# One token tile of four run ahead in plain float32 through the first half of a decoder block and gathered beside the rest; two tiles left dense

## The chip, the cores and the metric

One core of a Trainium2 chip. The time is the device time of one execution in microseconds. TensorE multiplies (a 128 x 128 array), VectorE and ScalarE work on 128-row tiles, GpSimd issues indirect DMAs (gathers of rows by an index), SyncE issues plain DMAs. Each engine runs its instructions in the order of the program and waits on semaphores for the others.

## The reference

512 tokens of width 1024 go through one block. The first half: adaLN modulation, an input projection to 7168 columns, four-head retention in chunks of 128 tokens, a spatial gating branch in chunks of 128, two output projections merged by gates, `w_out`, and the residual. The second half is PEER: each token picks 128 of 16384 experts (8 heads x 16) by two rounds of top-16, and sums single-neuron experts.

```python
q = (hb @ w_q).reshape(T, PEER_HEADS, 2, PEER_HALF)
s = jnp.einsum('thpc,hpnc->thpn', q, sub_keys)
sub_s, sub_i = lax.top_k(s, K)
cand = (sub_s[:, :, 0, :, None] + sub_s[:, :, 1, None, :]).reshape(T, PEER_HEADS, K * K)
top_s, top_i = lax.top_k(cand, K)
...
ue = expert_u[expert]
act = jax.nn.gelu(jnp.einsum('td,thkd->thk', hb, ue), approximate=False) * g
ve = expert_v[expert]
return jnp.einsum('thk,thkd->td', act, ve)
```

A token tile is 128 tokens. Retention and gating look back only, so the first tile needs no other tile.

## The kernel before

**First half.** All projections run over all four token tiles. A weight unit is 128 x 1024 float32 (512 KB). `Stream` loads units in order through SyncE into five `raw` buffers and splits each into a rounded part `wh` (ScalarE, L84) and a rest `wl` (VectorE, L87); `unit_mm` (L346) then makes three matmuls for each product (`wh`, `wl` and the activations' two parts), which come to nearly full float32. In the mode `tr` the 512 tokens are the columns, in the mode `nat` 512 weight columns are, once for each token tile.

**Second half.** Two methods share PEER's tokens. Dense: for a token, all 16384 expert scores are computed. `ahead` (L890) takes a 128-expert chunk of `uT` in plain float32 and spills the activations to memory (`sd`), `u_mm` does some chunks later in split form. The chosen experts' weights are spread by one-hot products (`onehots`, `wmm`) into a table `wd`, and in the last loop `a_make` multiplies activations and weights and `v_mm` (L1384) multiplies the result with the chunk's `v` rows. Gathered: for a token tile, `gather` (L1235) fetches, for each of the 128 choices, one `u` row and later one `v` row for all 128 tokens (512 KB each), and `consume` (L1251, L1256) does one VectorE pass over it, a dot product or an accumulation.

Before the change 320 tokens are dense (`TA`); the last tile (`accB`, 2 x 128 gathers) and 64 tokens of the first, folded into one 128-row set of 2 x 64 gathers (`accC`), are gathered: 384 in all, every one of them in the second half.

**What sets the order.** `plan()` writes the second half up to the last loop as a list of steps by estimated times of TensorE (`t["P"]`) and VectorE (`t["V"]`); `GPU` is the number of gathers credited for each ahead chunk. The last loop runs over 128 chunks in the list `items`; 88 have spilled scores, 40 are computed there. It spreads the gathers that are left (`left = NGT - ng[1]`) evenly over the iterations, with up to seven in flight, inside `a_make`, that is in VectorE's order ahead of the chunk's own work. The last four chunks are multiplied tile by tile, and each tile's norm and store follow.

Of the kernel before, what the change touches and what calls it, by code (L numbers as in the profile page):

```python
# [1 line left out]

# [21 lines left out]
H = 4  # L24
# [3 lines left out]
NA = 3  # L28
TP = 128 * NA
HC = 64  # L30
TA = TP - HC
# [6 lines left out]
GPU = 1.95  # L38
# [61 lines left out]
def plan():  # L100
# [4 lines left out]
    t = {"P": 0.0, "V": 0.0, "n": 0, "credit": 0.0, "go": False}  # L105

    def ahead():
        while pend and pend[0][0] <= t["P"]:
            _, st, c = pend.pop(0)
            steps.append(st)  # L110
            t["P"] += c
        steps.append(("U", t["n"]))
        t["n"] += 1
        t["P"] += 4.35
        if t["go"]:
            t["credit"] += GPU

    def pump():
        while (bq or dq) and t["V"] <= t["P"] + 6.0:
            if t["credit"] >= 1.0:  # L120
                t["credit"] -= 1.0
                steps.append(("gather",))
                t["V"] += 1.3
                continue
            st, c, after = (bq or dq).pop(0)
# [5 lines left out]
            if st[0] == "blist" and not t["go"]:  # L131
                t["go"], t["credit"] = True, -1.0
# [4 lines left out]
    def score(hp):  # L137
        steps.append(("score", hp))
        t["P"] += 0.9
        dq.append((("st1", hp), 3.2, None))  # L140
        if hp > 1 and hp % 2 == 0 or hp == 15:
            dq.append((("st2", (hp - 1) // 2), 2.7, None))
# [5 lines left out]
    ahead()  # L148
    ahead()
    steps.append(("chainB",))  # L150
    ahead()
    for g in range(4):
        for u in range(4):
# [3 lines left out]
            t["P"] += 5.2  # L157
# [8 lines left out]
    dq.append((("soft",), 4.0, None))  # L166
    for i in range(NA):
        dq.append((("list", i, 0), 3.4, None))
        dq.append((("list", i, 1), 4.2 if i else 4.8, (("listT", i), 0.8)))
# [15 lines left out]
def block_kernel(ctx: ExitStack, tc: tile.TileContext, a, out, dbg=None):  # L185
# [46 lines left out]

    big_p = ctx.enter_context(pool("big"))
    tmp2_cm = pool("tmp2"); tmp2 = tmp2_cm.__enter__()
    tmp_cm = pool("tmp"); tmp = tmp_cm.__enter__()

    def big(shape, dt, name):
        return big_p.tile(shape, dt, name=name, tag="big", bufs=6)
# [15 lines left out]
    def ada_dma(k, where=None, eng=None):  # L254

        ada_raw[k] = []
        for h in range(2):
            t = where[:, h] if where is not None else tmp.tile([128, 4, 256], F32, name="ada", tag="ada", bufs=4)
# [40 lines left out]
    def add_group(w, g):  # L299
        for u in range(4):  # L300
            ws.add(w[g, u])
# [16 lines left out]

# [20 lines left out]
    for i in range(PRE):  # L339
        ws.add(a["uT"][items[i][0]])  # L340
    for i in range(NCH):
        if PRE <= i + LA < NCH and items[i + LA][1]:
            ws.add(a["uT"][items[i + LA][0]])
        ws.add(a["v"][items[i][0] * 128:(items[i][0] + 1) * 128, :])

    def unit_mm(mode, u, wH, wL, sH, sL, targets, dds=(0, 1)):  # L346
# [5 lines left out]
        for ps, b in targets:  # L352
            ab = slice(b * 128, (b + 1) * 128)
            for dd in dds:
# [6 lines left out]
                else:  # L361
                    T.matmul(ps, wH[:, dd, ab], sH[:, d, :], start=st, stop=False)  # L362
                    T.matmul(ps, wH[:, dd, ab], sL[:, d, :], start=False, stop=False)  # L363
                    T.matmul(ps, wL[:, dd, ab], sH[:, d, :], start=False, stop=sp)  # L364

    def gemm(mode, sH, sL, evict, hooks=None, tiles=(0, 1, 2, 3)):
        banks = {}
        for u in range(4):
# [16 lines left out]
    ada_dma(1, stage[0][:, 1], nc.sync)
    ws.dma(2)
    for k in range(2, 6):
        ada_dma(k, stage[k // 2][:, k % 2], nc.sync)
        if k < 5:
            ws.dma(k + 1)  # L390
    dummy = cp.tile([128, 1], F32, name="dummy")
# [4 lines left out]
    for t in range(NT):  # L396
        scr = tmp2.tile([128, D], BF16, name="scr4", tag="t2", bufs=5)
        A.activation(scr, xn[:, t, :], AF.Square, accum_out=ss[:, t:t + 1])
    rsqrt(cp, rs, ss, NT, 1.0 / D, "rq")
    for t in range(NT):  # L400
        if t % 2:
            A.activation(xn[:, t, :], xn[:, t, :], AF.Copy, scale=rs[:, t:t + 1])
        else:
            V.tensor_scalar(xn[:, t, :], xn[:, t, :], rs[:, t:t + 1], None, op0=OP.mult)

    hH = big([128, ND, S], F32R, "hH")
    hL = big([128, ND, S], F32R, "hL")
    wsT = tmp.tile([128, 4, 128], F32, name="wsT")
    bsb = tmp.tile([128, 4, 128], F32, name="bsb")
    rope = tmp.tile([128, NT, 2, 64], F32, name="rope")  # L410

    def xT(d):
        ps = bank()
        for t in range(NT):
            T.transpose(ps[:, t * 128:(t + 1) * 128], xn[:, t, d * 128:(d + 1) * 128], ident)
        return ps

    def to_hT(d, ps):
        w = tmp2.tile([128, S], F32, name="ht", tag="t2", bufs=5)
        A.activation(w, ps, AF.Identity, bias=mod[:, 0, d:d + 1], scale=mod[:, 1, d:d + 1])  # L420
        A.copy(hH[:, d, :], w)
        V.tensor_tensor(hL[:, d, :], w, hH[:, d, :].bitcast(F32), op=OP.subtract)

# [6 lines left out]

    warm = bank()

    def warm_up(n):
        for _ in range(n):
            T.matmul(warm[:, 0:128], ones, ident, start=True, stop=True)
    warm_up(50)
# [23 lines left out]
    for d in range(ND):  # L460
        st_b(d + 1)
        st_a(d + 2)
        ws.split(d + 3)
        if d == 3:
            ws.dma(10)
        st_c(d + 1)
        if d == 0:
            banks0 = [(bank(), b) for b in range(4)]
            banks1 = [(bank(), b) for b in range(2)]
            ws.dma(6)  # L470
            for k in (6, 7):
                ada_dma(k, None, nc.sync)
                ws.dma(k + 1)
        if d % 2 == 0:
            wu = [ws.get(), ws.get()]
        for (wH, wL), bs in zip(wu, (banks0, banks1)):
            unit_mm("nat", d // 2, wH, wL, hH, hL, bs, dds=(d % 2,))
    lnr = big([128, 2, D], F32, "lnr")
    svg = big([128, NT, D], F32, "svg")
# [4 lines left out]
    nc.sync.dma_start(bsb, a["sgu_b"].to_broadcast([128, 512]).rearrange("p (g t) -> p g t", g=4))  # L484
    nc.sync.dma_start(gates[:, 0, :], a["b_ada"][2:3, :].to_broadcast([128, D]))
    nc.sync.dma_start(gates[:, 1, :], a["b_ada"][5:6, :].to_broadcast([128, D]))
    ws.dma(12)
# [6 lines left out]
    dump("hT", hH.bitcast(F32))  # L494
    dump("hTL", hL.bitcast(F32))
    for ps, b in banks0:
        ev_sv(0)(b, ps)
    for ps, b in banks1:
        ev_sv(1)(b, ps)
    gemm("nat", hH, hL, ev_sv(1), tiles=(2, 3))  # L500
# [22 lines left out]
    bgh = {u: [ada_bg] for u in range(4)}  # L523
# [3 lines left out]
    lrs = cp.tile([128, NT], F32, name="lrs")  # L527

    def ln_stats():
        for t in range(NT):  # L530
            st = tmp.tile([128, 2, 6], F32, name="st", tag="st", bufs=2)
            for i in range(2):
                V.bn_stats(st[:, i, :], svg[:, t, i * 512:(i + 1) * 512])
            V.bn_aggr(mv[:, t, :], st)
        rsqrt(cp, lrs, mv[:, :, 1], NT, 1.0, "rq")

    def ln_apply(t):
        v = svg[:, t, :]
# [4 lines left out]
    qk = big([128, 2, H, S], F32, "qk")  # L543

    def ev_rope(w):
        def f(b, ps):
            x = ps.rearrange("p (h d) -> p h d", h=H)
            x1, x2 = x[:, :, 0:64], x[:, :, 64:128]
            cb = rope[:, b, 0:1, :].to_broadcast([128, H, 64])
            sb = rope[:, b, 1:2, :].to_broadcast([128, H, 64])  # L550
# [9 lines left out]
            pend.append((w, b, r))  # L560
# [3 lines left out]
    def rope_tr():  # L564
        w, b, r = pend.pop(0)
# [3 lines left out]
        A.copy(qk[:, w, :, b * 128:(b + 1) * 128], ps.rearrange("p (h t) -> p h t", h=H))  # L569


# [3 lines left out]
    def mix(cc):  # L575
        g = cc // 2
        ps = bank()
        for t in range(NT):
            T.matmul(ps[:, t * 128:(t + 1) * 128], svg[:, t, cc * 128:(cc + 1) * 128], wsT[:, g, :],
                     start=True, stop=True)  # L580
        m = tmp2.tile([128, NT, 128], F32, name="mx", tag="t2", bufs=5)
        V.tensor_tensor(m, ps.rearrange("p (n t) -> p n t", n=NT), bsb[:, g:g + 1, :].to_broadcast([128, NT, 128]),
# [8 lines left out]
    def ev_u(g):  # L591
        def f(b, ps):
            cc = 4 * g + b
            u = tmp2.tile([128, S], F32, name="ug", tag="t2", bufs=5)
            A.activation(u, ps, AF.Gelu)
# [4 lines left out]
            if b == 3:  # L600
# [4 lines left out]
    gemm("nat", hH, hL, ev_rope(0), hooks={0: [ln_stats], 1: [lambda: ln_apply(0)], 2: [lambda: ln_apply(1)],  # L605
                                          3: [lambda: ln_apply(2)]})
# [1040 lines left out]
```

## Time and profile before

| | us |
|---|---|
| median of 3 runs | 1733.07 (1731.33 to 1735.44) |
| the profiled execution | 1731.39 |
| its span, first to last instruction | 1729.7 |
| TensorE busy | 1675.3 (97%) |
| VectorE busy | 1373.3 (79%) |
| ScalarE busy | 700.2 (40%) |
| GpSimd busy | 591.0 (34%) |

The stages by their first TensorE instruction: the dense first half to about 469 us, `w_out` and the second norm to 539, queries and ahead chunks to 880, one-hot products to 1068, then the last loop with its six prologue chunks, and from about 1686 us the last chunks and the final norm. The page's slices are of about 43 us each. DMA is the mean busy share of 16 DMA engines, beside it the bytes that they moved.

### The profile page before, as it was taken

The numbers are of one execution on the slowest core, as the hardware profiler recorded it, in microseconds if no ns is written. First come the engines' busy times: TensorE is split into PE (matmuls) and PEld (weight loads), VectorE is DVE, ScalarE is ACT, GpSimd is POOL, SyncE is SP. The second block draws the span as 40 slices with busy tenths as digits, with TensorE's granted clock in tenths as the row PEclk, the third lists the DMA queues.
The fourth block names the chain that finished last, engine by engine and source line by source line (L and its number), as shares of the span: only waits on it lengthen the run. The fifth ranks groups of instructions, "written<-read, shape, count | busy, mean of one in ns | idle before, by whom it ended". The sixth has DMA issues, their size and how long they took to land.

```text
span 1729.7 us, 23047 instructions
## 1 busy us (share of the span) xinstructions
PE 1675.3 (97%) x8029; PEld 1353.4 (78%) x8029; DVE 1373.3 (79%) x2712; ACT 700.2 (40%) x1140; POOL 591.0 (34%) x505
## 2 busy tenths in 40 slices
PE   9999999999999989999999988899999999999995
PEld 8888888888877877777777766788888888888873
DVE  7676763353553899999899977699999999899996
ACT  6532532234244343112357664334434444434334
POOL 0000110000000025666876554254444444454440
PEclk9999999999999999999999999999999999999997
DMA  9625662123334168999999999999999999999993
GB/s 376 239 98 171 228 222 74 61 85 103 120 125 154 60 214 327 410 396 409 350 357 381 400 392 389 363 368 393 381 398 379 407 391 381 405 382 396 372 354 116
DMA packets 138741, 502.83 MB, mean 291 GB/s; under 512 B 15648, under 2 KB 15680, under 8 KB 138496
## 3 DMA queue, kind: packets, MB, share of 16 engines
q0 software_dynamic: 70416, 259.85, 39.8%
q1 hardware_dynamic: 68208, 241.50, 36.9%
q8 instruction: 64, 1.05, 0.2%
q14 instruction: 53, 0.43, 0.1%
HBM read 460.89 MB, written 39.85 MB: 289 GB/s over the span
## 4 chain that ended last, share of the span: by engine, by line
PE 63%; DVE 24%; DMA 7%; issue 3%; ACT 2%; POOL 0%; SPq 0%; DVEq 0%; ACTq 0%; POOLq 0%
PE acc L1384 25%; PE mm L362 5%; PE mm L364 5%; PE mm L363 5%; PE mm L358 4%; PE mm L359 4%; PE mm L360 4%; DVE gw L1251 3%; PE mm L888 2%; PE mm L886 2%; PE mm L887 2%; DVE gwl L1251 2%; DVE gwh L1251 2%; DMA wd<-stg 2%; DMA gwl<-in_v_dram,eidx 2%
## 5 line engine op out<-in xcount | busy, mean ns | idle before, releaser
L87 DVE TENSOR_TENSOR wl<-raw,wh 128x1024 fp32r<-128x1024 f32 x268 | 326.0, 1221 | 143.1 <-ACT wh L84 140.0
L1384 PE MATMUL acc<-wh,ah 128*128 128x512 f32 x1280 | 375.8, 400 | 14.2 <-DVE ah L1365 14.2
L896 PE MATMUL mm<-h2F,raw 128*128 128x320 f32 (+2 forms) x1424 | 387.0, 432 | 0.0
L896 PEld LDWEIGHTS mm<-h2F,raw 128*128 128x128 f32 x1424 | 268.4, 191 | 107.3 <-issue 1.8
L84 ACT CAST wh<-raw 128x1024 fp32r<-128x1024 f32 x268 | 279.0, 1047 | 84.7 <-PE mm L360 39.4
L1384 PEld LDWEIGHTS acc<-wh,ah 128*128 128x128 f32 x1280 | 238.9, 189 | 78.3 <-issue 12.0
L1384 PE MATMUL acc<-wl,ah 128*128 128x512 f32 x768 | 244.7, 399 | 0.0
L1361 ACT CAST ah<-aw 128x320 fp32r<-128x320 f32 x128 | 59.0, 461 | 314.5 <-DVE aw L1359 310.7
L1384 PEld LDWEIGHTS acc<-wl,ah 128*128 128x128 f32 x768 | 145.9, 190 | 35.7
L1235 POOL DMA_INDIRECT gr<-in_v_dram,eidx x86 | 112.6, 1309 | 140.1 <-DVE accB L1256 122.1
L1235 POOL DMA_INDIRECT gr<-in_v_dram,ecidx x64 | 85.0, 1328 | 94.5 <-DVE wqb L1256 72.7
L1235 POOL DMA_INDIRECT gr<-in_u_dram,ecidx x64 | 83.6, 1306 | 88.4 <-DVE gr L1251 70.0
L1235 POOL DMA_INDIRECT gw<-in_u_dram,eidx x50 | 66.2, 1325 | 137.5 <-DVE eidx L1150 70.1
L1256 DVE SCALAR_TENSOR_TENSOR accB<-gr,dots,accB 128x1024 f32<-128x1024 f32 x86 | 110.2, 1281 | 1.3
L899 ACT ACTIVATE spl<-mm 128x320 f32<-128x320 f32 x88 | 38.0, 438 | 167.3 <-PE mm L896 105.2
L358 PE MATMUL mm<-wh,hH 128*128 128x512 f32 x256 | 102.3, 400 | 0.0
L888 PE MATMUL mm<-h2H,wl 128*128 128x320 f32 x320 | 98.9, 309 | 2.0 <-DVE wl L87 2.0
L886 PE MATMUL mm<-h2H,wh 128*128 128x320 f32 x320 | 98.9, 309 | 1.5 <-ACT wh L84 1.5
L360 PE MATMUL mm<-wh,hL 128*128 128x512 f32 x256 | 100.2, 391 | 0.0
L359 PE MATMUL mm<-wl,hH 128*128 128x512 f32 x256 | 100.2, 391 | 0.0
L887 PE MATMUL mm<-h2L,wh 128*128 128x320 f32 x320 | 98.9, 309 | 0.0
L1256 DVE SCALAR_TENSOR_TENSOR wqb<-gr,dotC,wqb 128x1024 f32<-128x1024 f32 x64 | 82.0, 1281 | 1.0
(343 smaller groups left out, 3148.6 us busy)
## 6 DMA issues: line engine op xcount, KB each, us to landing
raw<-in_uT_dram SPq DMA_DIRECT2D x128, 512.0 KB
raw<-in_v_dram SPq DMA_DIRECT2D x128, 512.0 KB
raw<-in_w_in_dram SPq DMA_DIRECT2D x60, 512.0 KB
wd<-stg POOLq DMA_DIRECT2D x10, 2048.0 KB
wqb<-wd SPq DMA_DIRECT2D x32, 640.0 KB
ada<-in_w_ada_dram POOLq DMA_DIRECT2D x28, 512.0 KB
sd<-spl POOLq DMA_DIRECT2D x44, 320.0 KB
sp<-sd SPq DMA_DIRECT2D x44, 320.0 KB
```

The source lines that it names most:

```text
L84: self.nc.scalar.copy(h, r)
L87: self.nc.vector.tensor_tensor(l, r, h.bitcast(F32), op=OP.subtract)
L358: T.matmul(ps, sH[:, d, ab], wH[:, dd, :], start=st, stop=False)
L359: T.matmul(ps, sH[:, d, ab], wL[:, dd, :], start=False, stop=False)
L360: T.matmul(ps, sL[:, d, ab], wH[:, dd, :], start=False, stop=sp)
L886: T.matmul(ps[:, p:q], h[:, d, :], h2H[:, d, cs], start=(d == 0), stop=False)
L887: T.matmul(ps[:, p:q], h[:, d, :], h2L[:, d, cs], start=False, stop=False)
L888: T.matmul(ps[:, p:q], l[:, d, :], h2H[:, d, cs], start=False, stop=(d == ND - 1))
L896: T.matmul(ps[:, p:q], r[:, d, :], h2F[:, d, HC + p:HC + q], start=(d == 0), stop=(d == ND - 1))
L1235: P.indirect_dma_start(out=r, out_offset=None, in_=a[tab], in_offset=bass.IndirectOffsetOnAxis(ap=ix[:, j:j + 1], axis=0))
L1256: V.scalar_tensor_tensor(acc, r, dt[:, j:j + 1], acc, op0=OP.mult, op1=OP.add)
L1384: T.matmul(accs[2 * t + e], x, y[:, e * 512:(e + 1) * 512], start=s0, stop=s1)
```

## The change

The first token tile goes alone through the first half before the other three. Its activations and the weights stay in plain float32: `gemm0` does one matmul for each product, with the tile's activations as stationary operand and 512 weight columns moving, on units that are not split. Its queries, scores and top-16 follow at once, and its gathers (2 x 128) are consumed by `bg_gather` after each weight unit of the other three tiles' first half (`GB1` = 1.4 each), and further on as before. The other tiles' first half has three tiles instead of four (`S3` = 384). In the second half two whole tiles are dense (`TA` = 256), the last tile is gathered as before, so there are 512 gathers. 80 chunks are spilled ahead and 48 computed in the last loop. Every second value chunk in the last loop stays unsplit (`vplain`) and is multiplied in plain float32. Weight units that the lone tile read are read again for the others.

```diff
-NA = 3
-TP = 128 * NA
-HC = 64
-TA = TP - HC
+N3 = NT - 1
+S3 = 128 * N3
+NA = 2
+TA = 128 * NA
...
-GPU = 1.95
+GPU = 1.4
+GB1 = 1.4
+VN = 2
...
-    t = {"P": 0.0, "V": 0.0, "n": 0, "credit": 0.0, "go": False}
+    t = {"P": 0.0, "V": 0.0, "n": 0, "credit": 0.0, "go": True}
...
+    add_two(a["w_in"][GSV:GSV + 2])
+    for g in (GSV, GSV + 1, GK, GQ, GV, GV + 1, GG, GG + 1, GU, GU + 1, GA, GA + 1):
+        add_group(a["w_in"], g, True)
...
+    vplain = [i % VN == 1 for i in range(NCH)]
...
+    def gemm0(s, evict, hooks=None, groups=2):
+
+        for g in range(groups):
+            ps = bank()
+            for u in range(4):
+                r = ws.get()
+                for dd in range(2):
+                    d = 2 * u + dd
+                    T.matmul(ps, s[:, d, :], r[:, dd * 512:(dd + 1) * 512], start=(d == 0), stop=(d == ND - 1))
+                for f in (hooks or {}).get((g, u), ()):
+                    f()
+            evict(g, ps)
...
+    gemm0(h0, ev_sv0, {(0, 1): [ada_bg], (0, 3): [ada_bg], (1, 1): [ada_bg]})
+    gemm0(h0, lambda g, ps: ev_rope(1, 0)(0, ps), {(0, 1): [ada_bg, lambda: ln_stats([0])], (0, 3): [lambda: ln_apply(0)]},
+          groups=1)
+    gemm0(h0, lambda g, ps: ev_rope(0, 0)(0, ps), {(0, 1): [ada_bg], (0, 2): [rope_tr]}, groups=1)
...
+    NGT = 4 * NJ
...
+        tab, j, G = ("u", "v")[i // NJ % 2], i % NJ, GT[i // (2 * NJ)]
...
+    def bg_gather():
+        if tq:
+            tq.pop(0)()
+        cr[0] = min(cr[0] + (0.6 if tq else GB1), 4.0)
+        gather_all()
+        while cr[0] >= 1.0 and ng[1] < ng[0]:
+            cr[0] -= 1.0
+            consume()
+            gather_all()
+    bg[0] = bg_gather
...
+    def v_mm(i, tiles, w, x, halves=(0, 1)):
         st, sp = (i == 0), (i == NCH - 1)
         for t in tiles:
-            if t == 0:
-                x = hl[:, TA:TA + 128]
-                runs = ((x, vh, st, False), (x, vl, False, sp))
+            o = slice(t * 128, (t + 1) * 128)
+            if vplain[i]:
+                runs = ((x[:, o], w, st, sp),)
             else:
...
-                runs = ((h, vh, st, False), (h, vl, False, False), (l, vh, False, sp))
+                h, l = x[:, 0, o], x[:, 1, o]
+                runs = ((h, w[0], st, False), (h, w[1], False, False), (l, w[0], False, sp))
```

On TensorE in the first half, at the value projection and the retention scores: before, all four tiles' split products (`hH`, `hL` are the two parts of the activations) go around the score products of all chunks.

```order
L358 MATMUL mm<-wh,hH 128x512
L359 MATMUL mm<-wl,hH 128x512
L360 MATMUL mm<-wh,hL 128x512
L651 MATMUL mm<-qk 128x512
L651 MATMUL mm<-qk 128x384
L651 MATMUL mm<-qk 128x256
L651 MATMUL mm<-qk 128x128
```

In the changed program the lone tile's piece of the same place stands some 800 instructions earlier, with unsplit units (`raw`) against the tile (`h`), its rotation (`rr`), scores (`qk`) and sums (`v`, `PT`) between them, and the sums of the modulation (`acc`).

```order
L416 MATMUL mm<-raw,h_104 128x512 x6
L632 MATMUL mm<-ident,rr 128x128 x4
L416 MATMUL mm<-raw,h_104 128x512 x4
L686 MATMUL mm<-qk_668 128x128 x4
L416 MATMUL mm<-raw,h_104 128x512 x6
L293 MATMUL mm<-ones,acc_905 128x1 x2
L416 MATMUL mm<-raw,h_104 128x512 x2
L698 MATMUL mm<-v_667,PT_953 128x256 x4
```

What moved: two matmuls stand for one weight unit where 24 stood, each unit is read a second time for the other three tiles, and each step of the tile follows the one before it closely.

On VectorE in the first half, at the gated output projection (`brb`) and the scores (`PT`): before, between the splits stand the modulation sums and the evictions.

```order
L273 TENSOR_TENSOR acc_2142<-acc_2142,acc_2143 128x256
L631 TENSOR_TENSOR brb<-mm,brb 128x512 x4
L87 TENSOR_TENSOR wl<-raw,wh 128x1024
L294 TENSOR_TENSOR gates<-mm,gates 128x256
L87 TENSOR_TENSOR wl<-raw,wh 128x1024 x3
L631 TENSOR_TENSOR brb<-mm,brb 128x512 x4
```

After, one or two gathered rows (`ga`, `gt`, `gwh`, `gwl` are the buffers; `h` the tile's activations) stand between one split and the next.

```order
L950 SCALAR_TENSOR_TENSOR gt,d_1824<-gt,h_1683 128x1024
L1078 TENSOR_TENSOR brb<-mm,brb 128x384 x4
L90 TENSOR_TENSOR wl<-raw,wh 128x1024
L950 SCALAR_TENSOR_TENSOR gwh,d_1824<-gwh,h_1683 128x1024
L90 TENSOR_TENSOR wl<-raw,wh 128x1024
L950 SCALAR_TENSOR_TENSOR gwl,d_1824<-gwl,h_1683 128x1024
```

What moved: gathers that the second half held stand here, 74 of them before the `w_out` projection of the three tiles.

On VectorE in the last loop: before, each chunk has one to three gathered rows among its own product (`aw`), rest (`ah`) and the splits of its weights.

```order
L1359 TENSOR_TENSOR aw<-sp_10854,wqb 128x320
L1251 SCALAR_TENSOR_TENSOR gr,dotC<-gr,h2C 128x1024
L1365 TENSOR_TENSOR ah<-aw,ah 128x320
L87 TENSOR_TENSOR wl<-raw,wh 128x1024 x2
L1359 TENSOR_TENSOR aw<-gs,wqb 128x320
L1251 SCALAR_TENSOR_TENSOR gr,dotC<-gr,h2C 128x1024 x3
L1365 TENSOR_TENSOR ah<-aw,ah 128x320
```

After:

```order
L1654 TENSOR_TENSOR aw<-sp_10577,wqb 128x256
L950 SCALAR_TENSOR_TENSOR gt,dB<-gt,h2B 128x1024 x2
L90 TENSOR_TENSOR wl<-raw,wh 128x1024
L1654 TENSOR_TENSOR aw<-gs,wqb 128x256
L950 SCALAR_TENSOR_TENSOR gt,dB<-gt,h2B 128x1024
L950 SCALAR_TENSOR_TENSOR gr,dB<-gr,h2B 128x1024 x3
L1665 TENSOR_TENSOR ah<-aw,ah 128x256
```

What moved: two to four rows stand in a chunk, every second chunk has no rest and no split of its value rows, and the loop begins with 202 of 512 gathers consumed, where it began with 170 of 384.

## Rows read from the trace of the kernel before

**Rows 1.** The page: span, busy us, DMA and bytes in 40 slices, packets.

```profile
span 1729.7 us, 23047 instructions
...
PE 1675.3 (97%) x8029; PEld 1353.4 (78%) x8029; DVE 1373.3 (79%) x2712; ACT 700.2 (40%) x1140; POOL 591.0 (34%) x505
...
DMA  9625662123334168999999999999999999999993
GB/s 376 239 98 171 228 222 74 61 85 103 120 125 154 60 214 327 410 396 409 350 357 381 400 392 389 363 368 393 381 398 379 407 391 381 405 382 396 372 354 116
DMA packets 138741, 502.83 MB, mean 291 GB/s; under 512 B 15648, under 2 KB 15680, under 8 KB 138496
```

**Rows 2.** Windows by stage: us, busy of each engine, clock, DMA share, GB/s.

```profile
60.00:469.00 409.00, 408.84 (x1879) 339.10 (x1878) 231.65 (x416) 137.04 (x191) 17.12 (x32) 1.00 0.37 127
539.00:880.00 341.00, 333.91 (x1372) 250.15 (x1371) 303.34 (x1215) 100.48 (x209) 167.61 (x145) 0.99 0.80 300
880.00:1068.00 188.00, 178.28 (x1154) 133.44 (x1152) 169.15 (x165) 120.24 (x134) 105.39 (x84) 0.99 1.01 384
700.00:820.00 120.00, 120.00 (x447) 84.72 (x446) 119.72 (x507) 21.94 (x63) 74.05 (x67) 1.00 1.02 404
1068.00:1686.00 618.00, 606.84 (x2923) 509.45 (x2924) 553.79 (x687) 248.49 (x454) 288.51 (x219) 1.00 0.99 384
1686.00:1730.00 44.00, 23.51 (x87) 17.40 (x85) 29.77 (x55) 19.50 (x35) 3.54 (x3) 0.78 0.33 115
```

**Rows 3.** Waits: engine, line, waited for, us, times, longest.

```profile
PE acc L1384 <- DVE ah L1365: 14.2, 9, 4.4
POOL gr L1235 <- DVE accB L1256: 131.9, 49, 16.4
```

**Rows 4.** TensorE: timeline (start, us), pieces of the chain, groups by form.

```profile
100.91 0.39 PE L364 MATMUL mm<-hH,wl 128*128 128x512 f32 x1
105.67 0.40 PE L364 MATMUL mm<-hH,wl 128*128 128x512 f32 x1
1200.27 0.31 PE L886 MATMUL mm<-h2H,wh 128*128 128x320 f32 x1
1202.33 0.31 PE L888 MATMUL mm<-h2H,wl 128*128 128x320 f32 x1
112.43 1.78 PE mm L579 x16
271.09 2.16 PE mm L651 x8
1150.29 15.18 PE acc L1384 x64
L1208 PE MATMUL mm<-ohA,ohB 128*128 128x128 f16 x320 | 39.2, 218 | 3.8 <-ACT stg L1210 1.6 <-ACT spl L899 1.5 <-DVE ohA L1193 0.7
```

**Rows 5.** DMA issues: count, KB each.

```profile
raw<-in_uT_dram SPq DMA_DIRECT2D x128, 512.0 KB
ada<-in_w_ada_dram POOLq DMA_DIRECT2D x28, 512.0 KB
wqb<-wd SPq DMA_DIRECT2D x32, 640.0 KB
sp<-sd SPq DMA_DIRECT2D x44, 320.0 KB
```

**Rows 6.** VectorE groups by form: busy us, mean ns, idle before.

```profile
L87 DVE TENSOR_TENSOR wl<-raw,wh 128x1024 fp32r<-128x1024 f32 x268 | 326.0, 1221 | 143.1 <-ACT wh L84 140.0
L1256 DVE SCALAR_TENSOR_TENSOR accB<-gr,dots,accB 128x1024 f32<-128x1024 f32 x86 | 110.2, 1281 | 1.3
L1256 DVE SCALAR_TENSOR_TENSOR wqb<-gr,dotC,wqb 128x1024 f32<-128x1024 f32 x64 | 82.0, 1281 | 1.0
L1251 DVE SCALAR_TENSOR_TENSOR gr<-gr,h2C 128x1024 f32<-128x1024 f32 x64 | 76.0, 1219 | 0.0
```

**Rows 7.** A window in which TensorE idles, columns as in rows 2.

```profile
640.00:680.00 40.00, 35.00 (x142) 26.14 (x141) 36.79 (x166) 13.98 (x32) 22.27 (x20) 0.91 0.80 278
```

More of the change, by code (lines that the diff above doesn't have):

```diff
@@ L1 @@
 from contextlib import ExitStack
+from types import SimpleNamespace
 import numpy as np
@@ L493, in block_kernel @@
     ws.ra, ws.sa = 5, 3
[L494 to L500, printed above, removed]
+    for g in range(2):
+        for ps, b in banks[g]:
+            ev_sv(g)(b, ps)
     ada_next = [8]
@@ new lines, in block_kernel, with ev_v0, scores0 @@
+    gemm0(h0, lambda g, ps: ev_rope(0, 0)(0, ps), {(0, 1): [ada_bg], (0, 2): [rope_tr]}, groups=1)
+    def ev_v0(g, ps):
+        A.copy(v0[:, half(g)], ps)
+    def scores0():
+        ps = bank()
+        for h in range(H):
+            T.matmul(ps[:, h * 128:(h + 1) * 128], qk0[:, 1, h, :], qk0[:, 0, h, :], start=True, stop=True)
+        PT0 = tmp2.tile([128, H, 128], F32, name="PT0", tag="t2", bufs=5)
+        V.tensor_tensor(PT0, ps.rearrange("p (h t) -> p h t", h=H), dec0, op=OP.mult)
+        PT["0"] = PT0
@@ new lines, in block_kernel, with pv0 @@
+    PT = {}
+    gemm0(h0, ev_v0, {(0, 0): [ada_bg], (0, 3): [rope_tr], (1, 1): [scores0]})
+    def pv0():
+        for hp in range(2):
+            ps = bank()
+            for hh in range(2):
+                h = 2 * hp + hh
+                T.matmul(ps[:, hh * 256:(hh + 1) * 256], PT["0"][:, h, :], v0[:, h * 256:(h + 1) * 256], start=True, stop=True)
+            A.copy(z0[:, half(hp)], ps)
+            for hh in range(2):
+                st = tmp.tile([128, 2, 6], F32, name="st", tag="st", bufs=2)
+                V.bn_stats(st[:, 0, :], ps[:, hh * 256:(hh + 1) * 256])
+                V.bn_aggr(hmv0[:, 2 * hp + hh, :], st[:, 0, :])
@@ new lines, in block_kernel, with score0 @@
+    l0 = lists_of(tk0, 1)
+    l0.e, l0.mx = (tk0.tile([128, 512], F32, name=n) for n in ("be", "bmx"))
+    s0 = {}
+    q0 = {}
+    def score0(g):
+        q = q0.pop(g)
+        ps = bank()
+        for i in range(4):
+            hp = 4 * g + i
+            kk_ = (keys0.a if hp < 8 else keys0.b)[:, hp % 8, :]
+            T.matmul(ps[:, i * 128:(i + 1) * 128], q[:, i * 128:(i + 1) * 128], kk_, start=True, stop=True)
+        s = (X[3], X[5])[g // 2][:, half(g % 2)]
+        A.copy(s, ps)
+        s0[g] = s
@@ L753, in ev_ret @@
         return f
+    gfree += [t0_tile("gt") for _ in range(2)]
     for g in range(2):
         gemm("tr", zH, zL, ev_ret(g))
+        if not g:
+            gdrop += ga + ["wh", "wl"]
+            gfree[:] = [b for b in gfree if not dropped(b)]
+    while any(dropped(b) for _, b in gt_t.values()):
+        consume()
+        gather_all()
+    bg[0] = lambda: None
     dump("mH", mH.bitcast(F32))
@@ L1323, in block_kernel @@
     dump("wd", wd)
-    while ng[1] < ng[0]:
+    gfree[:] = [x for x in gfree if not isinstance(x, str)]
+    gdrop += ["wh", "wl"]
+    while any(isinstance(b, str) for _, b in gt_t.values()):
         consume()
     ws.sa = 3
-    gfree, gdrop = [], []
     wx_cm.__exit__(None, None, None)
```

952 lines of the change are left out of this document (557 added, 395 removed).

## The prediction

> **What bounds the kernel now.** I read the page's busy shares and its forty slices first, then the windows of each stage, then the waits of the last stage, and only then single instructions. The page shows TensorE busy 97% of the span, with VectorE at 79%; the DMA line is what to look at: it is low from the second to the fourteenth slice and at nine tenths or more from the seventeenth to the last but one [rows 1]. The windows say the same by stage [rows 2]. In the dense first half (60 to 469 us) TensorE has no gap, VectorE works 232 of 409 us and the DMA engines run at a share of 0.37. From 700 to 820 us VectorE is busy 119.72 of 120 us and the DMA share is 1.02 at 404 GB/s. In the last loop (1068 to 1686 us) TensorE is busy 607 of 618 us, VectorE 554, and the DMA share is 0.99 at 384 GB/s. The waits there agree: TensorE lost 14.2 us to VectorE and nothing that is ascribed to a DMA, while GpSimd waited long for VectorE to free the buffer of the next gather [rows 3]. So TensorE sets the pace of the last loop, and the queues are full beside it without holding it up: two resources are at their end at once, a third close to it.
>
> **What TensorE saves and pays.** Prices first. A split matmul (three products of rounded operands) of 512 columns starts every 0.227 us (21 steps in 4.76 us), one of 320 columns every 0.147 us (14 steps in 2.06 us); a column is then worth (0.227 - 0.147) / 192 = 0.00042 us. Plain float32, which the trace records as two instructions for each matmul, costs about four times that a column: four score products of 1280 columns in all took 2.16 us, 0.00169 us a column; of 128 columns, eight took 1.78 us, 0.2225 us each. In the last loop a split product takes 15.18 / 64 = 0.237 us. A pair of one-hot products takes 39.2 / 320 = 0.12 us [rows 4].
>
> Up to the query projection (539 us before): in the split projections one token tile of four goes. 240 products of 512 columns disappear (54.4 us), 960 shrink from 512 to 384 columns (51.0 us). The lone tile adds 160 plain products of 512 columns (18 half-matrices of eight, and the two of the output projection): 160 x 512 x 0.00169 = 138.4 us, 128 plain query products of 128 columns, 28.5 us, and some 7 us of transposes and small products net. The two ahead chunks there shrink by 1.7 us. 539 - 105.4 + 138.4 + 28.5 + 7.0 - 1.7 = 606 us.
>
> What can be added to that: while the tile runs alone, it eats a weight unit of 512 KB every 1.73 us, 72 units, and 28 pieces of the modulation weights of the same size come through GpSimd's queue [rows 5]: 52.4 MB in about 139 us, 377 GB/s. The 404 GB/s of [rows 2] covers that, barely. Its steps also depend on each other: the key rotation waits on VectorE behind layer-norm work, and the routing of this tile lands on VectorE beside the first split gate group. Lower bound nothing; upper, weights at only the 300 GB/s of the query stage, 52.4 / 0.300 = 175, or 36 us, and some 10 more. I take 20 us: nearer the low end, since the rate needed is below what a row shows. So 626 us.
>
> The query and ahead stage with the one-hot stage (539 to 1068, 529 us): 86 ahead chunks of 2560 columns become 78 of 2048 (372 - 270 = 102 us saved), 384 projection products lose 128 columns (20.4 us), 16 score products (3.6 us) and 64 one-hot pairs (7.8 us) go: 134 us less, 395 us, with the waits of before kept. VectorE must follow: it worked 303 + 169 = 472 us there, of which 170 gathered rows at about 1.25 us [rows 6] were 212; 126 are left now (157 us), and of the other 260 I take a fifth off for the tile that left, 208: 365 us of 395. It fits. The DMA need (122 gathers, 94 units, the spilled activations and the expert weights) is 142 MB, 359 GB/s. It fits too. The last loop then begins at 626 + 395 = 1021 us.
>
> **The last loop.** TensorE's own part falls: 48 score chunks of 24 products at 256 columns (0.1205 us, 139 us), 64 split value chunks of 12 products (182 us), 64 plain ones of 4 (0.865 us each, 221 us): 542 us against the 607 of before. But the changed program, as built, has consumed only 74 gathers when the dense first half ends and 202 when the last loop begins; it leaves 310 of 512 to the last loop, where the kernel before left 214 (86, 64 and 64 in the groups of [rows 6]). The bytes: value rows 128 x 0.524 = 67.1 MB, score rows 48 x 0.524 = 25.2, expert weights 32 x 0.524 = 16.8, spilled activations 40 x 0.262 = 10.5, gathers 310 x 0.524 = 162.5, together 282 MB. The same count for the kernel before gives 67.1 + 21.0 + 21.0 + 14.4 + 112.2 = 236 MB, and 236 MB in 618 us is 381 GB/s, which the row confirms with 384. What rate will 282 MB get? Between the 384 of that loop and the 410 of the page's fullest slice: 734 to 688 us. I take 400, near the 404 of the window with a share of 1.02, since the loop of before also has stretches in which TensorE did not ask for more: 705 us. VectorE's part is 310 gathers at 1.27, 112 splits at 1.22 and some 77 us of small work, 608 us; so neither compute engine is the bound any more, the queues are. Gathers come late, VectorE stands behind them in order, the splits behind that stand, and TensorE waits. The TensorE time saved in this loop buys nothing.
>
> The Trainium skill (DMA: Bandwidth & Descriptors, Bandwidth) gives two ceilings, 435 GB/s for the ports and about 358 GB/s for memory to one core, and says that the second binds for loads. The 404 GB/s over 120 us speak against the second. By 358 the loop would take an estimated 788 us and the kernel end near 1856; by 435, 648 us and 1716.
>
> After the last gather the kernel before needed 44 us (1686 to 1730) for the last products, norm and store; the changed one has four chunks of two tiles there in place of three, and the same chain behind; I keep 44.
>
> **The sum.** 606 + 20 + 395 + 705 + 44 = 1770 us of span. The profiled execution took 1731.39 us for a span of 1729.7, and the median of the runs shown is 1733.07, so 3.4 us are added: **1773 us**, 2.3% slower. The gain of the design is real up to the last loop (47 us earlier); the loop then takes 87 us longer. A difference under 0.2% (3.5 us) could not be told from none.
>
> **Rivals.** *The queues are not the limit* (faster). Nothing before waits for a DMA in the loop, so 384 and 404 GB/s may be what was asked for and no ceiling, and the share near 1 only counts packets that wait for each other. Then VectorE paces the loop with 608 us: 606 + 20 + 395 + 608 + 44 = 1673, about 1676 us. It decides from 282 / (1730 - 1065) = 424 GB/s on; at that rate the kernel comes out even. For it: no DMA wait in [rows 3]. Against it: no slice of the page goes above 410, in stretches where different engines pace. The 435 of the Trainium skill would be this case.
>
> *The lone tile starves* (slower still). If units come at more than 1.73 us each, because five buffers and a second queue beside them do not give 377 GB/s, or the chain of one tile leaves TensorE waiting on VectorE at each step, the front pays 50 to 60 us where I put 20: 1803 to 1815 us. For it: plain chunks of 512 columns have no other tiles to hide a late eviction. Against: VectorE and ScalarE have half their time free there [rows 2].
>
> *TensorE's clock.* In the loop TensorE will idle about a quarter of the time. From 640 to 680 us it was busy 35 of 40 us and the granted clock was 0.91 of full speed [rows 7]; 542 us at 0.91 are 596, still under 705, so nothing changes. The Trainium skill (TensorE: Matmul & The Clock Gate, Part 1: The HAM clock gate) says that an idle array falls to 1.2 of 2.4 GHz. Were that so for the whole loop, its matmuls would take 1084 us and the kernel about 2150. No stretch of this trace with such a busy share shows it.
>
> **How the numbers follow.** Forecast 0.70, with a range of its own from 1742 (no stall in front, 410 GB/s: 606 + 395 + 688 + 44 + 3.4 = 1736, a little more since both at once are rare) to 1815 (36 us in front, 384 GB/s: 606 + 36 + 395 + 734 + 44 = 1815). Faster loop 0.13; starved tile 0.14; clock 0.03. To leave out no more than two in ten the range takes in the starved tile with a slow queue, and from below the forecast's own end: 1738 to 1832. Faster by over 0.2%: the first rival and a thin tail of the forecast, 0.14; the same, 0.03; slower, 0.83.
>
> **What would show it.** Right: in the last loop of the changed kernel a DMA share above 1, 395 to 410 GB/s, TensorE busy about 75%, VectorE about 86%, with VectorE's gathers waiting for indirect DMAs (none before); the last loop beginning near 1020 to 1040 us; the lone tile's stage near 140 to 160 us long with TensorE nearly full. Wrong: rates above 420 GB/s; VectorE full in the loop; a loop that starts after 1070 us, which would put the loss in front; or TensorE at a lower clock throughout.

## The result and the profile after

| | before | changed |
|---|---|---|
| median, us | 1733.30 (1731.33 to 1735.44, 4 runs) | 1792.15 (1789.45 to 1793.85, 4 runs) |
| ratio, 95% interval | | 1.0338 (1.0320 to 1.0356) |
| the profiled execution, span, us | 1729.7 | 1791.9 |

The changed kernel is 3.4% slower; 2.3% was forecast, and the time lies inside the range. On the page of the changed kernel, the lines that answer to [rows 1]:

```profile
span 1791.9 us, 22168 instructions
...
PE 1590.3 (89%) x7546; PEld 1241.4 (69%) x7546; DVE 1412.2 (79%) x2862; ACT 578.5 (32%) x912; POOL 750.5 (42%) x629
...
PEclk9999999999999899999999999998999898998898
DMA  8999767378568565799999999999999999999995
GB/s 339 381 358 373 285 220 238 129 258 294 186 237 317 187 231 194 232 375 413 395 380 397 395 372 381 408 408 377 408 408 408 408 408 408 408 403 387 409 406 211
DMA packets 168497, 601.84 MB, mean 336 GB/s; under 512 B 19072, under 2 KB 19072, under 8 KB 168256
```

TensorE has 85 us less to do than before (1590 for 1675), VectorE 39 us more, and the queues carry 602 MB for 503. What matters is the last line but one: from the 26th to the 39th slice it stands at 408 or 409 GB/s in ten of fourteen slices and never above. A rate that stands still like that looks like one that has come to its end; whether it has is what the first experiments ask. Only the 19th slice, in the stage of queries and ahead chunks, is higher, 413. So 408 is where this loop stops, not the most that the trace shows.

The windows by stage of the changed kernel, with the columns of [rows 2]: start, the lone tile, the three tiles' half in two pieces, `w_out` and the second norm, queries to one-hot products, the last loop up to about where its last gathers land, and the end.

```profile
0.00:61.00 61.00, 57.22 (x323) 49.85 (x324) 41.02 (x98) 40.20 (x69) 3.19 (x12) 0.97 0.92 349
61.00:239.00 178.00, 172.56 (x511) 88.27 (x509) 98.58 (x235) 42.65 (x80) 15.35 (x29) 1.00 0.91 335
239.00:350.00 111.00, 95.42 (x618) 89.80 (x617) 82.89 (x357) 38.69 (x71) 14.09 (x13) 0.95 0.59 196
350.00:599.00 249.00, 233.15 (x1195) 213.58 (x1194) 185.04 (x304) 80.34 (x106) 99.47 (x71) 0.97 0.71 251
599.00:659.00 60.00, 51.29 (x245) 42.18 (x244) 41.56 (x74) 28.43 (x48) 9.06 (x12) 0.91 0.49 168
659.00:1057.50 398.50, 383.49 (x2233) 346.42 (x2232) 371.11 (x1022) 181.65 (x292) 204.56 (x174) 0.98 0.93 352
1057.50:1765.00 707.50, 584.26 (x2399) 404.27 (x2400) 576.61 (x744) 158.59 (x234) 397.13 (x315) 0.91 1.02 402
1765.00:1792.00 27.00, 12.92 (x33) 7.08 (x31) 15.44 (x33) 7.96 (x15) 7.62 (x4) 0.78 0.20 79
```

Set beside the sum of the prediction: 659 us to the query projection where 626 were put, 398.5 where 395 were, 707.5 for the last loop where 705 were, and 27 at the end where 44 were. So the kernel enters its last loop 11 us earlier than before (1057.5 for 1068) and needs 734.5 us from there, where it needed 662.

In the last loop the waits of VectorE show what [rows 3] did not have: rows that VectorE waits for (engine, line, waited for, us, times, longest).

```profile
DVE gr L950 <- DMA gr<-in_u_dram,EB: 31.2, 34, 3.4
DVE accB L955 <- DMA gr<-in_v_dram,EB: 25.9, 29, 1.3
DVE gt L950 <- DMA gt<-in_u_dram,EB: 12.8, 15, 1.3
```

And the waits of TensorE there, behind VectorE's late rest (`ah`) and late splits (`wl`):

```profile
PE acc L1681 <- DVE ah L1665: 65.1, 15, 8.2
PE acc L1681 <- DVE wl L90: 39.7, 22, 5.3
```

One such place, the end of the loop on VectorE (start, us, engine, line; in brackets the idle time ahead and what ended it):

```profile
1741.07 1.28 DVE L955 SCALAR_TENSOR_TENSOR accB<-gr,dB,accB 128x1024 f32<-128x1024 f32 x1
1742.91 1.28 DVE L955 SCALAR_TENSOR_TENSOR accB<-gr,dB,accB 128x1024 f32<-128x1024 f32 x1 [0.56 <-DMA gr<-in_v_dram,EB]
1745.31 1.29 DVE L955 SCALAR_TENSOR_TENSOR accB<-gr,dB,accB 128x1024 f32<-128x1024 f32 x1 [1.11 <-DMA gr<-in_v_dram,EB]
1746.51 0.42 DVE L1665 TENSOR_TENSOR ah<-aw,ah 128x256 fp32r<-128x256 f32 x1
```

The rest that TensorE waits for stands behind three rows; two of them have not landed in time. In the wait list TensorE then waits for VectorE, and only VectorE's own list names the DMA.

### The profile page after: what moved, and what is told of

It is laid out like the page before. It is cut to its first block, busy times and chain, and to the rows that moved or that the text cites. A ratio compares the mean times of both kernels' runs of the same rounds, so it can differ in the third digit from the quotient of the medians.

```text
span 1791.9 us, 22168 instructions
## 1 busy us (share of the span) xinstructions
PE 1590.3 (89%) x7546; PEld 1241.4 (69%) x7546; DVE 1412.2 (79%) x2862; ACT 578.5 (32%) x912; POOL 750.5 (42%) x629
## 4 chain that ended last, share of the span: by engine, by line
DMA 23%; DVE 15%; issue 14%; POOL 8%; PE 6%; ACT 2%; POOLq 0%; DVEq 0%; ACTq 0%
DMA gt<-in_v_dram,EB 5%; DMA gr<-in_v_dram,EB 5%; DMA gr<-in_v_dram,E 4%; POOL gr L934 4%; POOL gt L934 3%; DMA wd<-stg 3%; DMA gr<-in_u_dram,EB 2%; DMA sd<-spl 2%; DVE acc L955 2%; DVE gt L950 1%; DVE wl L90 1%; PE mm L390 1%; PE acc L1681 1%; DMA gwl<-in_v_dram,E 1%; DVE gwh L950 1%
## 5 line engine op out<-in xcount | busy, mean ns | idle before, releaser
L1355 PE MATMUL mm<-h2F,raw 128*128 128x256 f32 (+1 forms) x1296 | 283.5, 380 | 0.3 <-ACT stg L1549 0.3
L1681 PE MATMUL acc<-wh,ah 128*128 128x512 f32 x512 | 197.2, 491 | 77.8 <-DVE ah L1665 65.1
L1681 PE MATMUL acc<-raw,aw 128*128 128x512 f32 x512 | 235.1, 601 | 1.0 <-DVE aw L1654 1.0
L1681 PEld LDWEIGHTS acc<-wh,ah 128*128 128x128 f32 x512 | 109.5, 221 | 127.5 <-DVE ah L1665 71.6
L1681 PEld LDWEIGHTS acc<-raw,aw 128*128 128x128 f32 x512 | 98.3, 195 | 98.8 <-issue 92.4
L1681 PE MATMUL acc<-wl,ah 128*128 128x512 f32 x256 | 94.9, 455 | 39.8 <-DVE wl L90 39.7
L1347 PE MATMUL mm<-h2H,wl 128*128 128x256 f32 x384 | 112.6, 293 | 10.8 <-DVE wl L90 10.8
L1345 PE MATMUL mm<-h2H,wh 128*128 128x256 f32 x384 | 120.8, 315 | 1.4 <-ACT wh L87 1.4
L1346 PE MATMUL mm<-h2L,wh 128*128 128x256 f32 x384 | 111.9, 292 | 0.0
L416 PE MATMUL mm<-raw,h 128*128 128x512 f32 x224 | 102.2, 598 | 3.8 <-DMA raw<-in_w_in_dram 3.8
```

Source lines behind the costliest of these rows:

```text
L416: T.matmul(ps, s[:, d, :], r[:, dd * 512:(dd + 1) * 512], start=(d == 0), stop=(d == ND - 1))
L1345: T.matmul(ps[:, p:q], h[:, d, :], h2H[:, d, cs], start=(d == 0), stop=False)
L1346: T.matmul(ps[:, p:q], h[:, d, :], h2L[:, d, cs], start=False, stop=False)
L1347: T.matmul(ps[:, p:q], l[:, d, :], h2H[:, d, cs], start=False, stop=(d == ND - 1))
L1355: T.matmul(ps[:, p:q], r[:, d, :], h2F[:, d, p:q], start=(d == 0), stop=(d == ND - 1))
L1681: T.matmul(accs[2 * t + e], s_, y[:, e * 512:(e + 1) * 512], start=s0_, stop=s1_)
```

## The experiments

Every experiment is a variation of the changed kernel, except the last one. "Query projection" is the time at which its first product starts (658.9 us in the changed kernel), "loop" the time from the first split score product (1056.8 us) to the end of the span (735 us). The kernel before took 1729.9 to 1732.5 us in these comparisons. A time without a ratio is that of one execution.

**What sets the last loop.** Theory: the queues, at about 408 GB/s. Rivals: VectorE, or TensorE.

*Fewer bytes, the same engine work.*

```diff
-        P.indirect_dma_start(out=r, out_offset=None, in_=a[tab],
+        if nloop[0] >= 0:
+            nloop[0] += 1
+        if nloop[0] < 16 or nloop[0] % 2:
+            P.indirect_dma_start(out=r, out_offset=None, in_=a[tab],
```

> In the last loop every second gathered row from the 16th on is not fetched; VectorE's pass over the old contents of the buffer stays, so all engine work is that of the changed kernel and some 79 of 282 MB are gone (about 147 to 150 transfers). Theory A (the queues at 408 GB/s set the loop): the transfers now need 203 MB / 0.408 = 498 us, VectorE's 592 us of work in loop and tail take over, and the stretch from 1057 us to the end falls from 734 to 630 to 660 us: 1690 to 1720 us in all. Theory B (VectorE's row of passes and splits sets the loop, the queues only look full): nothing changes, 1780 to 1795 us.

Measured: 1688.26 us. The loop's window in this kernel:

```profile
1057.50:1640.00 582.50, 534.53 (x2352) 370.46 (x2352) 553.47 (x723) 152.75 (x228) 251.30 (x164) 0.97 0.95 345
```

VectorE is now busy 95%, the rate has dropped to 345 GB/s. The time lies just under the first theory's range. With the same work on TensorE, VectorE and ScalarE the kernel is 104 us faster, so it was not their work that set the pace. GpSimd's work is not the same: it issues half of the gathers and is busy 251 us here, where it was 397. The two runs with more and with fewer rows left, further down, tell it from the transfers. The DMA share is still 0.95: by the share alone the queues would look as full as before.

*The same bytes, less VectorE work.*

```diff
+            cw = slice(0, nw_[0])
-            V.scalar_tensor_tensor(r, r, 1.0, G.h, op0=OP.mult, op1=OP.mult, accum_out=G.dots[:, j:j + 1])
+            V.scalar_tensor_tensor(r[:, cw], r[:, cw], 1.0, G.h[:, cw], op0=OP.mult, op1=OP.mult, accum_out=G.dots[:, j:j + 1])
...
+    nw_[0] = 64
```

> In the last loop each VectorE pass over a gathered row reads 64 of 1024 columns, all transfers stay: VectorE loses about 310 x 1.1 = 340 us of its work there. Theory A (queues): 282 MB / 0.408 = 691 us stay, and the time falls by at most 1%, 1775 to 1792 us. Theory B (VectorE): TensorE becomes the pace with its 542 to 600 us, and the time falls to 1660 to 1700 us.

Measured: 1787.04 us. The loop's window, and VectorE's longest waits in it:

```profile
1057.50:1740.00 682.50, 566.47 (x2361) 391.38 (x2362) 269.09 (x726) 157.25 (x228) 353.40 (x311) 0.92 1.02 405
```

```profile
DVE gr L952 <- DMA gr<-in_u_dram,EB: 103.8, 60, 4.0
DVE accB L958 <- DMA gr<-in_v_dram,EB: 78.2, 47, 3.2
```

VectorE's work is less than half (269 us; the changed kernel has 577 in a window 25 us longer), and 5 us of 1792 are gone. The time that it no longer works it waits for the rows.

*More of TensorE, less of VectorE.* All value chunks unsplit.

```diff
-    vplain = [i % VN == 1 for i in range(NCH)]
+    vplain = [True for i in range(NCH)]
```

> All 128 value chunks of the last loop stay unsplit, not 64: VectorE loses 64 splits and 64 rests (64 x (1.22 + 0.42) = 105 us), TensorE gains 64 x (3.46 - 2.84) = 39 us. Theory A (queues): the loop stays within 5 us, 1787 to 1797 us. Theory B (VectorE): 1690 to 1720 us. Theory C (TensorE): 1825 to 1835 us.

Measured: 1789.69 us, 1.0328 (1.0311 to 1.0346), the same as the changed kernel. *Less of TensorE.*

```diff
-                runs = ((h, w[0], st, False), (h, w[1], False, False), (l, w[0], False, sp))
+                runs = ((h, w[0], st, sp),)
```

> In the changed kernel the split value chunks of the last loop get one product instead of three (512 matmuls of 512 columns left out, 512 x 0.237 = 121 us of TensorE); VectorE's passes, splits and all transfers stay. Theory A (queues): 1785 to 1795 us. Theory B (TensorE's own time and waits still count in that loop): 1700 to 1770 us.

Measured: 1791.42 us. The loop's windows of these two kernels, all unsplit first:

```profile
1057.50:1745.00 687.50, 596.50 (x2121) 354.65 (x2122) 472.99 (x604) 76.12 (x107) 365.60 (x312) 0.93 1.02 403
```

```profile
1057.50:1745.00 687.50, 479.23 (x1880) 317.30 (x1879) 560.65 (x724) 155.62 (x230) 390.11 (x312) 0.87 1.02 404
```

TensorE works 597 us in the one and 479 us in the other, VectorE 473 and 561, and both kernels take the changed kernel's time. In that loop no work of TensorE or VectorE that was added or removed here counts; the bytes do.

**What a gathered row costs in the first half.** *None there.*

```diff
-GB1 = 1.4
+GB1 = 0.0
...
-        cr[0] = min(cr[0] + (0.6 if tq else GB1), 4.0)
+        cr[0] = min(cr[0] + GB1, 4.0)
```

> No gathered row is consumed after the weight units of the three tiles' first half (7 instead of 74 when it ends), 377 instead of 310 are left to the last loop. All theories on the loop by queues: 67 x 524 KB / 0.408 = 86 us more there. Theory A (the 31 us that TensorE idles between 239 and 599 us come from the gathered rows that stand ahead of the splits on VectorE and hold the buffers of the split weights): this stretch falls from 360 to 330 to 338 us, the whole is 1848 to 1858 us. Theory B (they come from the lone tile's routing and the evictions, which stay): it stays at 352 to 362 us, the whole 1870 to 1882 us.

Measured: 1877.12 us, 1.0830 (1.0789 to 1.0871), in the second theory's range. *More there.*

```diff
-GB1 = 1.4
+GB1 = 2.4
```

> 2.4 instead of 1.4 gathered rows are credited after each weight unit of the three tiles' first half: 123 instead of 74 are consumed when it ends, 261 instead of 310 are left to the last loop. By queues the loop loses 49 x 524 KB / 0.408 = 63 us. Theory A (gathered rows cost TensorE about 25 us for 67, that is 0.37 us each in that half): 18 us more there, 1747 us in all. Theory B (they lie beside it for nothing): 1729 us. Theory C (VectorE is full there, each row costs its whole 1.25 us): 61 us more, no change, 1785 to 1795 us. If VectorE and not the queues set the loop, the loop would also lose about 62 us, so this run alone does not tell these two apart.

Measured: 1774.86 us, 1.0244 (1.0203 to 1.0285), between the first theory's 1747 and the third's 1785: the rows cost 41 us in front and not 18 or 61. The loop behaves as the byte count says in both: it takes 826.5 us with 377 rows left and 669.6 with 261 (first row of each pair below is the three tiles' half with `w_out`, the second the loop to the end). None in front:

```profile
239.00:650.30 411.30, 376.89 (x2051) 343.84 (x2049) 231.81 (x596) 147.08 (x224) 22.83 (x27) 0.96 0.43 143
1047.50:1874.00 826.50, 621.72 (x2432) 425.89 (x2432) 687.74 (x851) 165.83 (x249) 491.94 (x389) 0.87 0.99 391
```

2.4 for each unit:

```profile
239.00:700.10 461.10, 393.17 (x2054) 353.54 (x2053) 365.54 (x832) 148.53 (x226) 188.00 (x145) 0.93 0.73 261
1101.70:1771.30 669.60, 580.87 (x2432) 399.30 (x2432) 536.79 (x727) 169.34 (x249) 337.14 (x271) 0.94 0.99 390
```

From 377 to 261 rows that is 157 us for 116 rows, 1.35 us each; 524 KB at 408 GB/s are 1.28 us. GpSimd's issues, or the time for which a gather holds its buffer, would go with the rows alone. But a row takes 2.2 us of the loop with 377 rows and 2.6 with 261, while most slices of both loops stand at 406 to 409 GB/s, and GpSimd is busy 60% and 50%. So it is the bytes.

In front the price is not even: from 7 to 74 rows the query projection moves from 650.3 to 658.9 us, 0.13 us a row; from 74 to 123 it moves to 700.1, 0.84 us a row. My first theory, that the rows make most of TensorE's idle time in that half, is refuted: without them 34 of the 40 us from 239 us to the query projection are still idle (411.3 less 376.9).

**Where that idle time comes from.** *The weights split three units ahead, not two.*

```diff
     gfree.append(t0_tile("gt"))
-    gfree += ["wh", "wl"]
-    ws.sa = 2
+    ws.sa = 3
```

> In the three tiles' first half the weights are split three units ahead instead of two, with the buffers that two gathered rows held; gathered rows have three buffers there instead of five; 73 instead of 74 are consumed when it ends. Theory A (TensorE idles there because bursts on VectorE, routing and rows, are longer than the cover of two units, 8.3 us): the half and the output projection lose 10 to 20 of their 49 us of idle time, 1772 to 1782 us. Theory B (VectorE has no time left there at all): no change, 1788 to 1795 us. Theory C (three buffers are too few and VectorE waits for rows): slower, above 1797 us.

Measured: 1780.56 us, 1.0276 (1.0259 to 1.0293); the query projection begins at 647.7, 11.2 us earlier. *The routing spread.*

```diff
+        tn[0] += 1
-        if tq:
+        if tq and tn[0] % 2:
             tq.pop(0)()
```

> The last seven pieces of the lone tile's routing run after every second weight unit of the three tiles' half instead of after every one; 69 instead of 74 gathered rows are consumed there, 315 instead of 310 are left to the last loop (5 x 1.28 = 6 us more there). Theory A (the routing burst makes most of the 15.6 us that TensorE idles from 239 to 350 us): 8 to 12 us less there, 1785 to 1790 us in all. Theory B (not the routing): 1796 to 1800 us.

Measured: 1789.39 us, 1.0340 (1.0311 to 1.0369); the query projection begins at 650.5, 8.4 us earlier, and 5 rows more in the loop take most of it back. Both times lie in the first theory's range. So part of the idle time is cover: the routing bursts are longer than what two split units hide. The changed kernel's own trace has such waits on TensorE, the first of them at the first product of the three tiles behind the lone tile's queries:

```profile
291.79 0.44 PE L388 MATMUL mm<-hH,wh 128*128 128x384 f32 x1 [0.66 <-ACT wh L87]
292.07 0.34 PE L389 MATMUL mm<-hL,wh 128*128 128x384 f32 x1
295.83 0.69 PE L390 MATMUL mm<-hH,wl 128*128 128x384 f32 x1 [3.42 <-DVE wl L90]
...
323.29 0.69 PE L390 MATMUL mm<-hH,wl 128*128 128x384 f32 x1 [3.54 <-DVE wl L90]
```

What VectorE does between the two splits ahead of the wait at 323 us is the lone tile's routing (`be`, `bk`, `E`), with the mixing product in front of it (lines between are left out):

```profile
314.04 1.23 DVE L90 TENSOR_TENSOR wl<-raw,wh 128x1024 fp32r<-128x1024 f32 x1
...
318.35 1.22 DVE L899 TENSOR_TENSOR be<-bib,IN 128x1024 bf16<-128x1024 bf16 x1
...
321.92 0.18 DVE L912 CAST E<-bk 128x32 uint32<-128x32 f32 x1
322.01 1.22 DVE L90 TENSOR_TENSOR wl<-raw,wh 128x1024 fp32r<-128x1024 f32 x1
```

The two waits do not have the same cure. The one at 296 us stands in both of these runs, 3.42 and 3.43 us long. The one at 323 us goes: with both cures put in (below) TensorE has no wait above 1.4 us between 297 and 340 us. And not all waits are VectorE's. TensorE's waits from 239 us to the query projection in the changed kernel name ScalarE's rounded part `wh` for 15 us beside VectorE's `wl` for 24:

```profile
PE mm L390 <- DVE wl L90: 15.5, 9, 3.5
PE mm L388 <- ACT wh L87: 11.2, 5, 4.4
PE mm L384 <- DVE wl L90: 8.0, 3, 4.1
PE mm L383 <- ACT wh L87: 3.7, 1, 3.7
```

*Three ahead and 2.4 rows.*

```diff
-GB1 = 1.4
+GB1 = 2.4
...
-    gfree += ["wh", "wl"]
-    ws.sa = 2
+    ws.sa = 3
```

> Three units ahead as above and 2.4 gathered rows for each unit: 123 consumed in that half, 261 left to the last loop. The loop loses 63 us as with 2.4 alone. Theory A (what 2.4 cost, 41 us, was mostly bursts longer than the cover): 1745 to 1762 us. Theory B (VectorE's sum): as 2.4 alone, 1770 to 1780 us. Theory C (three buffers): TensorE is no worse, but VectorE waits for rows and the half grows, above 1785 us.

Measured: 1826.27 us, 1.0544 (1.0526 to 1.0562). The third theory holds. The query projection begins at 748.1 us, where it began at 700.1 with 2.4 rows and five buffers. VectorE's waits for rows in the half, with five buffers (first line) and in this kernel:

```profile
DVE ga L950 <- DMA ga<-in_u_dram,E: 7.8, 9, 2.0
...
DVE ga L950 <- DMA ga<-in_u_dram,E: 63.2, 35, 4.5
DVE gt L950 <- DMA gt<-in_u_dram,E: 22.5, 16, 4.3
```

**A better point?** *The routing spread and 1.8 rows; and, with the two edits shown above, the routing spread and three ahead.*

```diff
-GB1 = 1.4
+GB1 = 1.8
...
+        tn[0] += 1
-        if tq:
+        if tq and tn[0] % 2:
             tq.pop(0)()
```

> Routing after every second unit and 1.8 gathered rows for each unit, splits two ahead, five buffers: 86 rows consumed when the three tiles' half ends, 298 left to the last loop instead of 310 (12 x 1.28 = 15 us less there). Theory A (the cost of a row in front is small as long as VectorE has time left, and rises from there on: 0.13 us each up to 74, 0.84 each on the way to 123): 1773 to 1779 us. Theory B (all rows above 74 cost 0.84): 10 us are given back, 1782 to 1787 us.

> Routing after every second unit and splits three ahead, 1.4 rows: 68 rows consumed when the half ends, 316 left (6 x 1.28 = 8 us more in the last loop than in the changed kernel). Theory A (the two cures act on different idle time): the query projection begins 11 + 8 us earlier, 1780 us. Theory B (both take the same idle time away): it begins 11 us earlier, 1786 to 1790 us. In neither case does the kernel come near the kernel before, which would take 1733 us: the bytes after the first half would have to fall by some 19 MB more than any of these cures gives back.

Measured: 1785.5 us, 1.0318 (1.0285 to 1.0350), and 1778.12 us, 1.0267 (1.0248 to 1.0285). With 1.8 the half and `w_out` take 424.9 us where they took 411.5 with the routing spread alone, 0.79 us for each of 17 rows more, so the price rises already at about 70 rows, not at some later point: the second theory. With three ahead the query projection begins at 639.8, 19 us earlier than in the changed kernel: the two cures act on different idle time. TensorE still idles 24 us between 239 us and there (400.8 less 376.3), where the changed kernel has 40. Of the kernels that do all the work it is the best but for 2.4 rows in five buffers, and 47 us behind the kernel before.

**Was the loop of before at both ends?** In the kernel before, two of three products of both whole tiles left out in every second value chunk.

```diff
                 runs = ((h, vh, st, False), (h, vl, False, False), (l, vh, False, sp))
+                if i % 2:
+                    runs = ((h, vh, st, sp),)
```

> The same 512 matmuls left out of the last loop of the kernel before (two of the three products of both whole tiles, in every second value chunk). TensorE's 607 us there become 486. Theory A (queues full beside TensorE, as the prediction has it): 236 MB / 0.408 = 579 us take over from 618, with VectorE's 554 below: 1692 to 1708 us. Theory B (VectorE or TensorE alone): 554 to 560 us for the loop, 1665 to 1680 us. Theory C (something else paces that loop): 1725 us or more.

Measured: 1713.59 us, 16 us less for 121 us of TensorE work left out. None of the three ranges holds it. The loop in three windows:

```profile
1068.00:1300.00 232.00, 200.80 (x963) 169.50 (x964) 203.99 (x229) 95.27 (x172) 105.82 (x83) 0.96 1.01 392
1300.00:1500.00 200.00, 176.90 (x838) 146.74 (x836) 190.89 (x286) 86.55 (x159) 100.01 (x77) 0.97 1.02 405
1500.00:1669.00 169.00, 142.22 (x629) 116.38 (x630) 157.56 (x174) 65.30 (x120) 82.12 (x61) 0.93 0.99 385
```

The rate rises to 405 in the middle window, with VectorE at 95% there; at both ends of the loop it is 385 to 392, with VectorE at 88% and 93%. So something stood right behind TensorE in the loop of before, with some 17 us to spare. Queues and VectorE are both close to their end: from 1327 to 1541 us the rate is the 408 of the changed kernel. But VectorE waits for no gathered row in this whole loop, and what TensorE waits for is VectorE's rest. The window and the wait:

```profile
1327.00:1541.00 214.00, 186.91 (x868) 154.46 (x867) 203.48 (x300) 89.74 (x165) 108.04 (x82) 0.96 1.03 408
```

```profile
PE acc L1386 <- DVE ah L1365: 78.4, 43, 4.6
```

The wait lists thus speak for VectorE and not for the queues. They do not prove it, since VectorE's work (552 of 601 us) leaves some room, and no run takes work from VectorE or bytes from the queues in this kernel.

## Why the prediction was right, and where it was off

*The last loop.* Right in mechanism and size: 284 MB by the windows (282 counted) at 402 GB/s, 707.5 us for 705. What was to be seen is there: a share of 1.02, a rate of 395 to 410, VectorE waiting for rows (96 us, none in the loop of before) and busy 82% for 86. TensorE was busy 83% and not 75%: at a granted clock of 0.91 its work came to 597 us up to the end (584 and 13), where the terms make 542, or 596 at 0.91 as the third rival had it. That this costs nothing was said there, and the run with fewer products, at 0.87, shows it. The faster rival is refuted by the two runs on bytes and passes: its VectorE-paced loop appears only once the bytes are gone.

The Trainium skill (DMA: Bandwidth & Descriptors, Bandwidth) puts memory to one core at about 358 GB/s and the ports at 435. The same section gives the 358 as the share of a core when both cores of a pair load at once, and 425 as measured on one core alone; the prediction took the 358 without that condition. The 402 GB/s over 707 us lie between the two ceilings, and the plateau of 408 stands above the one and below the other; no run here reached 435.

*The lone tile's stall.* This term was mis-sized, and its place was wrong. I put 20 us, with an upper end of 46, and looked for them in the lone tile's stage, in weights that come too late. That stage has 5.4 us of idle TensorE (178.0 less 172.6); it is 178 us long and not 140 to 160, because 75 split products and the small ones stand in it beside the 160 plain products. By the windows TensorE idles 49 us up to 659, where it idled 6 up to 539 before: 16 beside the routing (239 to 350), 16 in the rest of the three tiles' half, 9 in `w_out`. So of the 33 us that the front took beyond 626, 23 are idle time beyond the 20 that I put, and 10 are TensorE's own work (610 us where the terms make 600). 33 us more than put comes out like the second rival's price (50 to 60 where I put 20), but not by its mechanism.

What I missed: two buffers of the split weights are lent to the gathers, the splits run two units ahead instead of three, and bursts on VectorE are no longer covered. I took from [rows 2] that VectorE has half its time free there, and did not look at the longest burst in front of a split. The runs show this for 16 of the 40 us between 239 us and the query projection, those that three units ahead and the spread routing take away together. The rows themselves account for little, since 34 us stay without them. Where the other 24 us come from is open.

*The stage between.* 398.5 for 395: right.

*The end.* 27 us for 44, by luck on the right side: I carried over the time of the kernel before, counted from 1686 us, while its last gathers there were consumed only about 1696 us; in the changed kernel the last rows are consumed until 1771 us, beside TensorE's last chunks. This 17 us took back half of the stall's error, so the whole came out nearer than its parts. The loop begins at 1057.5 us, later than the 1020 to 1040 that was to show the prediction right, and short of the 1070 that was to put the loss in front.

*Two slips.* The 14.2 us that [rows 3] gives for TensorE's wait go up to the end of the kernel; 8.6 of them lie in the loop. And the sum of 1815 at the upper end leaves out the 3.4 us.

*The trade as a whole.* The change takes TensorE time (85 us) and pays in bytes (99 MB), in a kernel whose loop already ran at 384 of 408 GB/s. The kernel before with 121 us of TensorE work left out gains 16 us.

## What to carry to other kernels

Before work is moved from an engine to the queues, count the bytes of the stage that will hold them and divide by the highest rate that any window of the trace sustains; an engine's gain is only worth what the next resource has to spare there. Move the bytes to the stage whose rate is low, but price them by the engine that consumes them in order: the first rows were nearly free (0.13 us), the next cost 0.8. And when a buffer is lent, look at the longest burst that its depth used to cover, not at the sum of the work.

## What was unexpected of the hardware

The DMA share does not say whether the queues hold the kernel up: 0.95 at 345 GB/s when VectorE set the pace, 0.99 at 384 with TensorE at the pace, 1.02 at 402 to 405 when the queues did, and 1.02 at 404 in a stretch of the kernel before in which TensorE was never idle [rows 2]. The rate, steady over many slices at 408, was the better sign, but no proof: the last run above holds 408 GB/s for 214 us while VectorE waits for no row. What told the two apart was VectorE's own wait list, and taking the bytes away.
